# The last mixer's output weights: low halves by a VectorE subtraction instead of an adding transfer, and loads in another order

## The chip, the cores and the metric

The kernel runs on one core of one Trainium2 chip. The metric is the device time of one execution in microseconds (us), as the median of several runs. All five engines of the core have their own queue of instructions and run beside one another: PE (TensorE, the matmuls), DVE (VectorE), ACT (ScalarE), POOL (GpSimd) and SP (SyncE, which here only starts transfers). Each engine takes its queue in order; an instruction that must wait holds up all that stands behind it on that engine.

## The reference

Two blocks over a sequence of 256 rows of width 1024, all in float32: first a block with a pooling and gated-delta mixer and an MLP, then two layers, one with a spatial gating mixer and one with an RWKV-7 mixer, each followed by a squared-relu MLP of hidden width 4096. The change lies in the last steps of the RWKV-7 mixer:

```python
def _rwkv7_mixer(h, mu, w_rkv, ..., ln_g, ln_b, w_o, v_first, v_mix):
    ...                                             # r, k, v, decay, a, g from projections of h
    y = _wkv7_scan(r_h, heads(decay), k_h, v_h, kk, kk * heads(a))   # state recurrence over time
    y = (y - mean(y)) * rsqrt(var(y) + GN_EPS)      # per head of 64
    y = y * ln_g + ln_b
    bonus = sum(r_h * k_h * r_k, axis=-1) * v_h
    y = (y + bonus) * g
    return y @ w_o                                  # [256, 1024] x [1024, 1024]

x = x + y;  x = x + _squared_relu_mlp(_rmsnorm(x, g_ffn), w1, w2);  return _rmsnorm(x, final_g)
```

## The kernel before

A matmul that must be exact in float32 is made of three passes: each operand is split into a high half (a cast to float32r on ACT) and a low half (the rest), and `mm3` (lines 225 to 227) issues high x high, low x high and high x low into the same PSUM bank. So a weight tile of 128x1024 is ready only when its low half is.

There are two ways to make a low half. `split` (line 213 casts, line 217 subtracts) has DVE compute `src - high`. With `lo="x"`, and in `w_out`, `rest` does it instead: ACT writes `-high` into the low tile (line 221), and a transfer that POOL issues adds the raw weights to it (line 222).

`rwkv` holds the mixer. Four windows of 64 time steps (w = 0 to 3) and two halves of the heads (hb = 0, 1) are worked through in five steps: `step(s, fills)` runs `state` (lines 1637 to 1661), `solve` (lines 1669, 1671), `update` (lines 1679 to 1687) and `output` (lines 1693, 1697) of window s for hb = 0 and of window s - 1 for hb = 1, and calls the functions in `fills[0..3]` after state, solve, update and output. These functions are what else there is to do: `fin(d, n)` (the normalisation and gating of row tile d, column half n, lines 1705 to 1718, ended by the four transposes and the split in `half_xt`, lines 246 to 250), `gate_in(n)` (load of the gate weights and of two vectors, lines 1561 to 1564), `gate(n, t)` (their matmuls and products, lines 1575 to 1577), `w_out` (one 128-row tile of the output weights) and `out_mm(t, k, first)` (the output product of row tile t with weight tile k; PSUM tile `ra`).

`w_out` is called eight times, k = 0 to 7. At even k it starts the load of two tiles (`load_as`, line 184, 1 MB) into a raw tile. Raw tiles (`raw`) take turns in two buffers, with those of `gate_in`, so that a load starts when the last reader of the raw tile two before it is done. Each k then has a home for its halves: the pool `wz` for k = 0 and 1 (behind the v weights, whose matmuls are `v`), the tiles `gain` and `sq` for k = 2, the tile `lv` for k = 3 and 4 (it holds the window matrices of w = 0 and 1, last read by `output` of window 1 in step 2), the tile `EL` for k = 5 (last read by `update` of window 1, step 2), `mix` for k = 6 (last read by `update` of window 2, step 3) and `lx` for k = 7 (last read by `output` of window 2, step 3). In the rows all of k = 2, 5 and 6 are called `wo`, k = 0 and 1 `rwoh` and `rwol`, and the raw tiles `rwo`.

The order on each engine is fixed when the program is built: a planner takes the calls in the order of the code as their priority, and pulls a later one forward where it holds that one ready earlier. So the matmuls of `out_mm` and `gate` stand among those of the recurrence on PE, and all casts among the copies of the recurrence on ACT.

After step 4, `early` adds the product to the residual (`add_res`, line 343), the sums are transposed (`m3x`, line 379) and split (lines 382, 385), and the last MLP starts with the matmuls `m3h`; its weights (`m3u`, `m3d`) go through the same raw buffers and through memory that the mixer leaves.

Of the kernel before, what the change touches and what calls it, by code (L numbers as in the profile page):

```python
# [10 lines left out]
F32 = mybir.dt.float32  # L11
# [113 lines left out]
def tile_two_blocks(ctx: ExitStack, tc: tile.TileContext, a: dict):  # L125
    nc = tc.nc
    act, dve, pool, pe, sync = nc.scalar, nc.vector, nc.gpsimd, nc.tensor, nc.sync
# [36 lines left out]
    def acc(i, name):  # L164
        return pa.tile([P, 1024], F32, tag=f"acc{i}", name=name)
# [4 lines left out]
    def raw(name):  # L170
        wpick[1] += 1
        w_ = extra[-1][1] if extra and extra[-1][1] and wpick[1] % 2 and not wpick[2] else wr
        return w_.tile([P, 2048], F32, tag="raw", name=name)
# [22 lines left out]
    def split(src, name, lo=dve, at=None, of=None):  # L196
        shape = list(src.shape)
        n = 1
        for s in shape[1:]:
            n *= s  # L200
        if at is None:
            wpick[0] += 1
            w_ = of or (extra[-1][0] if extra and wpick[0] % 2 and not wpick[2] else wp)
            h = w_.tile([P, 1024], F32R, tag="wh", name=name + "h")
            l = w_.tile([P, 1024], F32R, tag="wl", name=name + "l")
        else:
            x = area(at, [2, D], F32R)
            h, l = x[:, 0], x[:, 1]
        hv, lv = h[:, :n], l[:, :n]
        if len(shape) == 3:  # L210
            hv = hv.rearrange("p (a b) -> p a b", a=shape[1])
            lv = lv.rearrange("p (a b) -> p a b", a=shape[1])
        act.copy(hv, src)  # L213
        if lo == "x":
            rest(lv, hv, src)
        else:
            lo.tensor_tensor(out=lv, in0=src, in1=hv.bitcast(F32), op=ALU.subtract)  # L217
        return hv, lv

    def rest(lv, hv, src):  # L220
        act.activation(out=lv, in_=hv.bitcast(F32), func=AF.Copy, scale=-1.0)
        pool.dma_start(out=lv.bitcast(F32), in_=src, accum_op=ALU.add)

    def mm3(out, lh, ll, rh, rl, first, last):
        pe.matmul(out, lhsT=lh, rhs=rh, start=first, stop=False)  # L225
        pe.matmul(out, lhsT=lh, rhs=rl, start=False, stop=False)  # L226
        pe.matmul(out, lhsT=ll, rhs=rh, start=False, stop=last)  # L227
# [913 lines left out]
    def rwkv(fed, early, cols, mu, hcol, hka, laf):  # L1141
        NP, CH = 8, 64
        half = 0.5 * DECAY
        with tc.tile_pool(name="wz", bufs=2) as wz, tc.tile_pool(name="rw", bufs=1) as bp:
# [75 lines left out]
            with tc.tile_pool(name="rwm2", bufs=2) as m2, tc.tile_pool(name="rwm", bufs=1) as mp:  # L1220
# [288 lines left out]
                def dense():  # L1509
                    for c in (2, 3):  # L1510
                        yield from r_proj(c)
                    q2 = ps("bon")
                    for k in range(NK):
                        for t in range(2):
                            o = t * 16 + k * 2
                            pe.matmul(q2[:, o:o + 2], lhsT=pr[:, k, t * P:(t + 1) * P], rhs=sel[:, k],
                                      start=True, stop=True)
                    dve.tensor_copy(bon.rearrange("p t k -> p (t k)"), q2[:, :32])
                    G1 = xp.tile([P, NK * (T + 1)], F32, tag="xh", name="G1", bufs=2)
                    V1 = xp.tile([P, NK * (T + 1)], F32, tag="xl", name="V1", bufs=2)  # L1520
                    G1, V1 = [x[:, :2 * D].rearrange("p (t m) -> p t m", t=2) for x in (G1, V1)]
                    ac = [acc(t, f"v{t}") for t in range(2)]
                    gv.extend((G1, V1, ac))
                    for k, t in v_proj(0):
                        yield 1
                        if t == 0:
                            gram(k // 2, k % 2)
                            continue
                        if k < 6:
                            turn_bk(k // 2, k % 2)  # L1530
                    v_out(0)
# [13 lines left out]
                def v_out(n):  # L1545
                    G1, V1, ac = gv
                    m = slice(n * 512, n * 512 + 512)
                    for t in range(2):
                        act.copy(DV[0][0:64, t, m], ac[t][0:64, m])
                        act.copy(DV[1][64:128, t, m], ac[t][64:128, m])  # L1550
                        dve.tensor_tensor(out=V1[:, t, m].rearrange("p (h v) -> p h v", v=64),
                                          in0=ac[t][:, m].rearrange("p (h v) -> p h v", v=64),
                                          in1=bon[:, t, 8 * n:8 * n + 8].unsqueeze(2).to_broadcast([P, 8, 64]),
                                          op=ALU.mult)
# [3 lines left out]
                def gate_in(n):  # L1558
                    s = slice(512 * n, 512 * n + 512)
                    w = raw(f"gb{n}")  # L1560
                    sync.dma_start(out=w[:, 0:512], in_=a["rwkv_g_lora_b_2"][0][:, s])
                    lng, lnb = w[:, 512:1024], w[:, 1024:1536]
                    sync.dma_start(out=lng, in_=a["rwkv_ln_g_2"][0][s].partition_broadcast(P))
                    sync.dma_start(out=lnb, in_=a["rwkv_ln_b_2"][0][s].partition_broadcast(P))
                    gates[n] = (lng, lnb) + split(w[:, 0:512], "lgb", of=wp)

                def gate(n, t):
                    G1, V1, _ = gv
                    s = slice(512 * n, 512 * n + 512)
                    lng, lnb, wh, wl = gates[n]  # L1570
                    if not t:
                        gates["q"] = acc(0, "lg")
                    q = gates["q"][:, 512 * t:512 * t + 512]
                    mm3(q, gfh[:, t * P:(t + 1) * P], gfl[:, t * P:(t + 1) * P], wh, wl, True, True)
                    EN[KP["vl"][2 * n + t]].tensor_tensor(out=V1[:, t, s], in0=V1[:, t, s], in1=lnb, op=ALU.add)
                    dve.tensor_mul(V1[:, t, s], V1[:, t, s], q)
                    dve.tensor_mul(G1[:, t, s], lng, q)

                gv = []
                early_fill, late_fill = dense(), v_proj(1)  # L1580
# [141 lines left out]
                wo, wo_raw, lw = [], [], []  # L1722
# [24 lines left out]
                def w_out():  # L1747
                    k = len(wo)
                    if k % 2 == 0:
                        wo_raw.append(load_as(a["rwkv_w_o_2"][0], k * P, f"rwo{k}"))  # L1750
                    w = wo_raw[-1][:, k % 2]
                    if homes[k] is None:
                        wo.append(split(w, "rwo", "x", of=wz))
                    else:
                        h, l = homes[k]()
                        act.copy(h, w)
                        rest(l, h, w)
                        wo.append((h, l))

                def out_mm(t, k, first):  # L1760
# [5 lines left out]
                def step(s, fills):  # L1766
                    todo = [(w, hb) for hb, w in ((0, s), (1, s - 1)) if 0 <= w < 4]
                    for i, stage in enumerate((state, solve, update)):
                        for x in todo:
                            stage(*x)  # L1770
                        for f in fills[i]:
                            f()
                    output(todo)
                    for f in fills[3]:
                        f()
                    todo = [(w + 1, hb) for w, hb in todo if w < 3] + [(0, 1)] * (s == 0)
                    if todo:
                        before(todo)

                c0, c1 = corners(0), corners(1)  # L1780
                some = lambda g, n=1: [lambda: next(g, None)] * n
                rest_of = lambda g: [lambda: [None for _ in g]]
                for _ in c0:
                    next(late_fill, None)
                before([(0, 0)])
                both_fill = [some(c1, 2) + some(late_fill, 2)] * 3
                step(0, both_fill + [rest_of(c1) + rest_of(late_fill) + [lambda: v_out(1), lambda: gate_in(0)]])
                yh, yl = xt_tiles("y")
                f00, f01, f10, f11 = [fin(d, n) for d in both for n in both]
                step(1, [[lambda: gate(0, 0)], [lambda: gate(0, 1), lambda: gate_in(1)], [w_out], [w_out]])  # L1790
                step(2, [some(f00) + [lambda: gate(1, 0)], some(f00) + [lambda: gate(1, 1)],
                         some(f00) + [w_out], some(f00)])
                step(3, [some(f01) + [w_out], some(f01) + [w_out], some(f01) + [w_out], some(f01) + [w_out, w_out]])
                ac = [acc(0, "ra0")]
                outs = lambda t, ks, first: [lambda k=k: out_mm(t, k, first) for k in ks]
                step(4, [some(f10) + outs(0, [0], 0), some(f10) + outs(0, [1], 0), [], some(f10) + outs(0, [2], 0)])
# [21 lines left out]
    with tc.tile_pool(name="lp", bufs=1) as lp:  # L1818

        def area(tag, shape, dt=F32):  # L1820
            return lp.tile([P] + shape, dt, tag=tag, name=tag)
# [83 lines left out]
```

## Time and profile before

| | |
|---|---|
| median of 3 runs | 1082.83 us (1080.8 to 1084.26) |
| profiled execution, its own time | 1082.16 us |
| its span, first to last instruction | 1080.4 us |
| granted TensorE clock, mean | 0.983 |
| busy: PE, DVE, ACT, POOL | 1043.5, 716.3, 567.3, 59.0 us |
| moved by transfers that add (q0) | 8.39 MB in 2304 packets |

Times in the rows are in us from the start of the span unless marked ns. A timeline row gives start, duration, engine, line, operation, what it writes and reads, and in brackets how long the engine had been idle before it and what ended that. In the chain of work each piece is what the next one waited for. A granted clock of 1.00 is TensorE at 2.4 GHz, 0.50 is 1.2 GHz; a value between is a mean over a stretch with both.

### The profile page before, as it was taken

The page shows a single profiled execution, that of the slowest core. Times are in us where ns is not written, and L with a number is a line of the kernel's source. Part 1 is how long each engine was busy: PE and PEld are TensorE (multiplying, and loading weights), DVE is VectorE, ACT ScalarE, POOL GpSimd, SP SyncE. Part 2 cuts the span into 40 slices and gives each one's busy share as a digit, 9 for nine tenths or more (in the row PEclk, how much of TensorE's full clock was granted, in tenths as well). Part 3 has the DMA queues.
Part 4 walks back from the last instruction along what each step waited for, and adds up shares of the span by engine and source line. Part 5 has one row for each costly group of instructions (what it writes and reads, how often), then busy time and mean ns, then how long its engine had stood idle before and what let it go on. Part 6 is the DMA issues. An engine that isn't in the chain of part 4 may idle for free.

```text
span 1080.4 us, 18579 instructions
## 1 busy us (share of the span) xinstructions
PE 1043.5 (97%) x7626; PEld 932.3 (86%) x7626; DVE 716.3 (66%) x1201; ACT 567.3 (53%) x840; POOL 59.0 (5%) x94
## 2 busy tenths in 40 slices
PE   8999999999999999999999999999999789999996
PEld 6899878988899999889989998998777569999985
DVE  5989665555658886666685556998936465555565
ACT  5744464454456554555464546864656445444452
POOL 3100000000002000000000001022001100000000
PEclk9999999999999999999999999999999799999999
DMA  8343186555565645556575561456624874566531
GB/s 247 120 157 118 46 314 214 182 181 177 174 198 153 197 155 174 178 166 190 161 248 188 191 192 36 109 148 142 152 50 118 188 221 159 192 195 187 187 134 39
DMA packets 124465, 177.76 MB, mean 165 GB/s; under 512 B 6766, under 2 KB 100955, under 8 KB 124124
## 3 DMA queue, kind: packets, MB, share of 16 engines
q1 hardware_dynamic: 121930, 168.11, 49.0%
q0 software_dynamic: 2304, 8.39, 4.1%
q8 instruction: 60, 0.98, 0.4%
q14 instruction: 25, 0.20, 0.1%
q10 hardware_dynamic: 146, 0.07, 0.0%
HBM read 167.12 MB, written 1.05 MB: 156 GB/s over the span
## 4 chain that ended last, share of the span: by engine, by line
PE 82%; DVE 9%; DMA 4%; ACT 2%; issue 2%; POOL 1%; SPq 0%; ACTq 0%; POOLq 0%; DVEq 0%
PE m3h L227 3%; PE m3h L226 3%; PE m1a L225 3%; PE m3h L225 3%; PE m1a L227 3%; PE m1a L226 3%; PE m1h L226 3%; PE m2h L226 3%; PE m1h L227 3%; PE m2h L227 3%; PE m1h L225 3%; PE m2h L225 3%; PE m2a L225 3%; PE m2a L226 3%; PE m2a L227 3%; PE m3a L225 3%
## 5 line engine op out<-in xcount | busy, mean ns | idle before, releaser
L225 PE MATMUL m3h<-m3xh,m3uh 128*128 128x256 f32 x256 | 72.6, 284 | 1.9 <-ACT m3xh L382 1.9
L227 PE MATMUL m3h<-m3xh,m3ul 128*128 128x256 f32 x256 | 73.0, 285 | 0.5 <-DVE m3ul L217 0.5
L225 PE MATMUL m1h<-m1xh,m1uh 128*128 128x256 f32 x256 | 73.4, 287 | 0.0
L217 DVE TENSOR_TENSOR m3ul<-m3u,m3uh 128x1024 fp32r<-128x1024 f32 x32 | 39.2, 1226 | 51.1 <-ACT m3uh L213 51.1
L226 PE MATMUL m3h<-m3xl,m3uh 128*128 128x256 f32 x256 | 73.0, 285 | 0.0
L226 PE MATMUL m1h<-m1xl,m1uh 128*128 128x256 f32 x256 | 71.8, 281 | 0.2 <-DVE m1xl L385 0.2
L227 PE MATMUL m2h<-m2xh,m2ul 128*128 128x256 f32 x256 | 71.7, 280 | 0.0
L227 PE MATMUL m1h<-m1xh,m1ul 128*128 128x256 f32 x256 | 71.7, 280 | 0.0
L226 PE MATMUL m2h<-m2xl,m2uh 128*128 128x256 f32 x256 | 71.6, 280 | 0.0
L225 PE MATMUL m2h<-m2xh,m2uh 128*128 128x256 f32 x256 | 71.5, 280 | 0.0
L217 DVE TENSOR_TENSOR m1ul<-m1u,m1uh 128x1024 fp32r<-128x1024 f32 x32 | 39.2, 1225 | 45.1 <-ACT m1uh L213 45.0
L213 ACT CAST m3uh<-m3u 128x1024 fp32r<-128x1024 f32 x32 | 33.4, 1047 | 56.5 <-PE m3h L226 50.7
L217 DVE TENSOR_TENSOR m2ul<-m2u,m2uh 128x1024 fp32r<-128x1024 f32 x32 | 39.1, 1225 | 35.8 <-ACT m2uh L213 35.8
L213 ACT CAST m1uh<-m1u 128x1024 fp32r<-128x1024 f32 x32 | 33.7, 1053 | 52.3 <-PE m1h L226 50.5
L213 ACT CAST m2uh<-m2u 128x1024 fp32r<-128x1024 f32 x32 | 33.5, 1050 | 47.9 <-PE m2h L226 45.8
L217 DVE TENSOR_TENSOR m2dl<-m2d,m2dh 128x1024 fp32r<-128x1024 f32 x32 | 39.2, 1225 | 26.1 <-ACT m2dh L213 26.1
L217 DVE TENSOR_TENSOR m3dl<-m3d,m3dh 128x1024 fp32r<-128x1024 f32 x31 | 38.0, 1225 | 24.9 <-ACT m3dh L213 24.9
L217 DVE TENSOR_TENSOR m1dl<-m1d,m1dh 128x1024 fp32r<-128x1024 f32 x31 | 37.9, 1224 | 22.0 <-ACT m1dh L213 22.0
L225 PEld LDWEIGHTS m3h<-m3xh,m3uh 128*128 128x128 f32 x256 | 49.0, 192 | 2.8 <-ACT m3xh L382 2.2
L213 ACT CAST m2dh<-m2d 128x1024 fp32r<-128x1024 f32 x32 | 33.6, 1050 | 33.4 <-PE m2a L227 29.9
L213 ACT CAST m1dh<-m1d 128x1024 fp32r<-128x1024 f32 x31 | 32.5, 1047 | 35.3 <-PE m1a L227 24.4
L213 ACT CAST m3dh<-m3d 128x1024 fp32r<-128x1024 f32 x31 | 32.6, 1052 | 33.4 <-PE m3a L227 31.6
(691 smaller groups left out, 3513.4 us busy)
## 6 DMA issues: line engine op xcount, KB each, us to landing
m1u<-in_w_up_dram SPq DMA_DIRECT2D x16, 1024.0 KB, 5.5
m1d<-in_w_down_dram SPq DMA_DIRECT2D x16, 1024.0 KB, 5.0
m2u<-in_ffn_w_dram SPq DMA_DIRECT2D x16, 1024.0 KB, 6.4
m2d<-in_ffn_w_dram SPq DMA_DIRECT2D x16, 1024.0 KB, 5.2
m3u<-in_ffn_w_dram SPq DMA_DIRECT2D x16, 1024.0 KB, 5.5
m3d<-in_ffn_w_dram SPq DMA_DIRECT2D x16, 1024.0 KB, 5.1
win<-in_w_in_dram SPq DMA_DIRECT2D x10, 1024.0 KB, 5.3
sv<-in_sgu_w_in_dram SPq DMA_DIRECT2D x8, 1024.0 KB, 5.8
```

Of the source, the lines that this page charges most:

```text
L213: act.copy(hv, src)
L217: lo.tensor_tensor(out=lv, in0=src, in1=hv.bitcast(F32), op=ALU.subtract)
L225: pe.matmul(out, lhsT=lh, rhs=rh, start=first, stop=False)
L226: pe.matmul(out, lhsT=lh, rhs=rl, start=False, stop=False)
L227: pe.matmul(out, lhsT=ll, rhs=rh, start=False, stop=last)
```

## The change

Two lines change how the eight low halves are made, and the lists of fills change when `w_out` is called:

```diff
-                        wo.append(split(w, "rwo", "x", of=wz))
+                        wo.append(split(w, "rwo", of=wz))
                     else:
                         h, l = homes[k]()
                         act.copy(h, w)
-                        rest(l, h, w)
+                        dve.tensor_sub(l, w, h.bitcast(F32))
                         wo.append((h, l))
...
-                step(0, both_fill + [rest_of(c1) + rest_of(late_fill) + [lambda: v_out(1), lambda: gate_in(0)]])
+                step(0, both_fill + [rest_of(c1) + rest_of(late_fill) + [lambda: v_out(1), lambda: gate_in(0), w_out, w_out]])
...
-                step(1, [[lambda: gate(0, 0)], [lambda: gate(0, 1), lambda: gate_in(1)], [w_out], [w_out]])
-                step(2, [some(f00) + [lambda: gate(1, 0)], some(f00) + [lambda: gate(1, 1)],
-                         some(f00) + [w_out], some(f00)])
-                step(3, [some(f01) + [w_out], some(f01) + [w_out], some(f01) + [w_out], some(f01) + [w_out, w_out]])
+                step(1, [[lambda: gate(0, 0)], [lambda: gate(0, 1), lambda: gate_in(1)], [w_out], []])
+                step(2, [some(f00) + [lambda: gate(1, 0)], some(f00) + [lambda: gate(1, 1)], some(f00), some(f00) + [w_out]])
+                step(3, [some(f01) + [w_out], some(f01) + [w_out], some(f01), some(f01) + [w_out, w_out]])
```

By k: before, k = 0 and 1 come after update and output of step 1, k = 2 after update of step 2, and k = 3 to 7 in step 3 (one each after state, solve and update, two after output). After the change k = 0 and 1 come after output of step 0, k = 2 after update of step 1, k = 3 after output of step 2, k = 4 and 5 after state and solve of step 3, k = 6 and 7 after its output. With that the raw tiles follow one another as gate 0, weights 0 and 1, gate 1, weights 2 and 3, 4 and 5, 6 and 7; before, both gates came first.

## Rows read from the trace of the kernel before

**Rows 1.** Page, part 4: shares of the chain of work, by engine

```profile
PE 82%; DVE 9%; DMA 4%; ACT 2%; issue 2%; POOL 1%; SPq 0%; ACTq 0%; POOLq 0%; DVEq 0%
```

**Rows 2.** Windows: length; busy PE, PEld, DVE, ACT, POOL; clock; DMA share; GB/s

```profile
805.00:840.00 35.00, 33.39 (x413) 27.12 (x414) 21.94 (x52) 21.90 (x35) 4.53 (x5) 1.00 0.44 102
840.00:848.60 8.60, 3.64 (x37) 2.82 (x32) 2.23 (x4) 3.37 (x4) 0.02 (x1) 1.00 0.81 201
848.60:867.10 18.50, 16.81 (x79) 12.21 (x77) 7.21 (x18) 8.85 (x13) 3.44 (x4) 0.54 0.84 199
867.10:889.50 22.40, 17.90 (x82) 13.16 (x82) 16.18 (x36) 9.57 (x21) 0.00 (x0) 1.00 0.74 236
889.50:893.10 3.60, 3.60 (x20) 3.60 (x18) 2.13 (x10) 2.18 (x6) 0.00 (x0) 0.53 0.00 0
```

**Rows 3.** Chain of work from 838 to 885: start, us, what

```profile
838.10 9.53 DMA lv<-rwo
...
859.87 10.59 DMA lx<-rwo
...
877.87 7.01 DMA m3u<-in_ffn_w_dram
```

**Rows 4.** Timeline of PE: waits for low halves, recurrence groups, a gate matmul

```profile
815.02 0.50 PE L225 MATMUL lg<-lgbh,gfh 128*128 128x512 f32 x1
...
826.99 1.10 PE L1693 MATMUL PD<-tBK,lv 128*64 128x64 f32 x16
...
840.13 0.92 PE L1693 MATMUL PD<-tBK,lx 128*64 128x64 f32 x13
842.58 0.50 PE L226 MATMUL ra<-wo,yh 128*128 128x512 f32 x1 [1.52 <-DMA wo<-rwo]
...
847.67 0.50 PE L226 MATMUL ra<-lv,yh 128*128 128x512 f32 x1 [3.44 <-DMA lv<-rwo]
```

**Rows 5.** Timeline of ACT: casts and negations among the recurrence's copies

```profile
807.07 0.58 ACT L1661 COPY xx<-PD 64x512 f32<-64x512 f32 x1
...
821.46 1.99 ACT L213 CAST rwoh<-rwo 128x1024 fp32r<-128x1024 f32 x2
823.36 2.00 ACT L221 ACTIVATE rwol<-rwoh 128x1024 fp32r<-128x1024 f32 x2
...
845.23 1.04 ACT L1756 CAST lv<-rwo 128x1024 fp32r<-128x1024 f32 x1 [6.56 <-DMA rwo<-in_rwkv_w_o_dram]
...
849.15 1.19 ACT L1697 COPY tBK<-PD 64x512 f32<-64x512 f32 x2
```

**Rows 6.** Groups by line, 800 to 890: count, busy us, mean ns, idle before

```profile
L221 ACT ACTIVATE wo<-wo 128x1024 fp32r<-128x1024 f32 x3 | 3.1, 1049 | 0.0
...
L217 DVE TENSOR_TENSOR m3ul<-m3u,m3uh 128x1024 fp32r<-128x1024 f32 x3 | 3.7, 1224 | 3.4 <-ACT m3uh L213 3.4
```

**Rows 7.** Transfers by issue, 725 to 900: count, KB each, median us to landing

```profile
wo<-rwo POOLq DMA_DIRECT2D x3, 512.0 KB, 9.1
...
rwo<-in_rwkv_w_o_dram SPq DMA_DIRECT2D x4, 1024.0 KB, 6.7
...
gb<-in_rwkv_g_lora_b_dram SPq DMA_DIRECT2D x2, 256.0 KB, 2.6
```

**Rows 8.** Timeline of SP's queue: a gate load, the first two weight loads

```profile
793.46 0.33 SPq L1561 DMA_DIRECT2D gb<-in_rwkv_g_lora_b_dram  x1
...
814.46 0.38 SPq L184 DMA_DIRECT2D rwo<-in_rwkv_w_o_dram  x1
...
825.07 0.38 SPq L184 DMA_DIRECT2D rwo<-in_rwkv_w_o_dram  x1
```

**Rows 9.** Timeline of DVE: the second gate weights' low half; the last fin

```profile
800.45 0.69 DVE L217 TENSOR_TENSOR lgbl<-gb,lgbh 128x512 fp32r<-128x512 f32 x1
...
867.22 0.69 DVE L1705 TENSOR_REDUCE gm<-tBK 128x8 f32<-128x512 f32 x1 [0.56 <-ACT tBK L1697]
...
878.37 0.69 DVE L250 TENSOR_TENSOR yl<-yt,yh 128x512 fp32r<-128x512 f32 x1 [1.37 <-ACT yh L249]
```

## Prediction, written before the changed kernel was timed

> **What bounds the kernel now.** I read the shares of the chain of work first: PE holds 82% of it [rows 1], so time is won where PE waits or runs slowly, and nowhere else. Then the windows around the last mixer's end [rows 2], cut where the clock changes. From 805 to 840 us PE is busy 33.39 of 35.00 us: nothing to win there but 1.61. From 840.0 to 848.6 it is busy 3.64 of 8.60, and from 848.6 to 867.1 it is busy 16.81 of 18.50 but at a granted clock of 0.54, mostly 1.2 GHz. From 867.1 to 889.5 it is busy 17.90 of 22.40 at full clock, and from 889.5 to 893.1 the clock is at 0.53 again [rows 2]. So two kinds of loss stand side by side:
> - waits from 840.0 to 867.1: 8.60 - 3.64 + 18.50 - 16.81 = 6.65 us;
> - the low clock: 16.81 us of work that at full clock would be 16.81 x 0.54 = 9.1, so 7.7 us; and 3.60 x 0.47 = 1.7 in the short stretch at 889.5.
>
> Third, the chain and the timelines say what ended the waits. The chain runs through two adding transfers, 9.53 and 10.59 us from POOL's issue to landing [rows 3]. PE stood 1.52 and 3.44 us before the first matmul that reads a low half [rows 4]. ACT stood 6.56 us before the cast of k = 4, for a load whose raw buffer was still being read by the adding transfers of k = 0 and 1; behind that cast stood the copies of step 3's output, which ran at 849.15 although their matmuls were done by 841.05 (840.13 + 0.92) [rows 4, 5]. So step 4 of the recurrence began 8 us late on account of the weights. After 867.22 the last `fin` takes to 879.06 (878.37 + 0.69) [rows 9], with PE short of work at its end; this is a chain of small steps that the change leaves.
>
> **The change part by part.** *Removed:* eight ACT negations, 8 x 1.049 = 8.4 us [rows 6]; eight adding transfers, each about 9.1 us from issue to landing [rows 7]. *Added:* eight DVE subtractions of the same shape as those of the MLP's weights, 8 x 1.224 = 9.8 us [rows 6]. A low half now follows its cast by 1.2 us, instead of a negation, an issue and a transfer, 1.05 + 9.1 us and more. Also the raw buffer is free after the subtraction, so the next load no longer waits for the adding transfer.
>
> *Moved, by k.* The load of k = 0 and 1 takes the place that the second gate load had in the buffers, so it starts at about 793.46 [rows 8] and is there by 800.2 (6.7 us to landing [rows 7]). Its halves must wait for the v matmuls, to about 805, and are done near 809. The load of k = 2 and 3 can start when these are done or behind the gate load on SP's queue, near 815 instead of 825.07 [rows 8]; k = 2 is ready near 825. k = 3 must wait for its home until 826.99 + 1.10 = 828.1 [rows 4]. The load of k = 4 and 5 waits for the gates' last product, about where the load at 825.07 started [rows 8], or a few us later; it lands near 835. That of k = 6 and 7 follows the subtraction of k = 3, near 831, and lands near 839; their homes come free at 840 to 841 [rows 4]. So all eight low halves are there by about 846, where the last one before landed at 859.87 + 10.59 = 870.46 [rows 3]. Then neither PE's waits for low halves nor ACT's wait of 6.56 has a cause left.
>
> *What is late next.* From 841 on there are two limits. One is PE's own work: 3.64 + 9.1 + 17.90 = 30.6 us at full clock for what lay between 840.0 and 889.5 [rows 2], which would end at 870.6. The other is the chain: from 841.05 the two copies of output, 1.19; state's matmuls, about 2.7 (an estimate from 1.10 for a group of 16 [rows 4], for 16 such and 8 wider ones); then copy, solve, copy, output, copy, 3 x 0.58 + 2 x 1.1 [rows 4, 5], with hand-overs of 0.1: about 849.4; the last `fin`, 11.84 us from its start to its end before [rows 9], at 861; the last product, then the sums, transposes and splits. This too comes to about 871. Two limits that close together don't hide each other fully: of the 6.65 + (22.40 - 17.90) = 11.15 us of waits I leave 4.2, most of it in the tail.
>
> *What is added to the path.* Four terms that the trace of before doesn't show:
> - The casts of k = 0 and 1 now stand at about 805, ahead of the copy that ACT began at 807.07 [rows 5] and that the recurrence waits for. Cost 0 to 2.0 us (two casts, the 1.99 of [rows 5]); I take 1.0, since PE had other matmuls to run. The place they leave, 821.46 to 825.36 [rows 5], gives ACT 4 us, which PE, full there, can hardly use: 0 to -1.6, taken as 0.
> - The second gate load now waits for the first gate's buffer, to 814.46, where before it was issued at 793.46 [rows 8]. Landing 2.6 [rows 7], a cast and a subtraction of 0.69 [rows 9] bring its low half near 818.5 to 819.5, where PE reached its first gate matmul at 815.02 [rows 4]. Behind that matmul the recurrence of step 2 is queued on PE, and behind the product on DVE the state's additions. Cost 0 to 4.5; I take 0.5, because these matmuls can stand later in PE's order at no loss.
> - The subtractions of the last three k fall among the small DVE steps of the last two `fin`: 0 to 3 x 1.224 = 3.7; I take 0.5, since DVE was busy only 9.44 of the 27.10 us from 840.0 to 867.1 [rows 2].
> - The loads start earlier and meet less other traffic: 0.
>
> *Sum.* Waits 11.15 - 4.2 = 6.95; low clock 7.7; half of the 1.7 at 889.5, as that stretch follows a wait of PE that I only shorten: 0.85; less 2.0 for the added terms: 13.5 us. The profiled execution took 1082.16, which is 0.67 under the median of the runs; the sum is made against the former: 1082.2 - 13.5 = 1068.7.
>
> On the clock there is a rule to weigh. The 7.7 us rest on a low clock through 848.6 to 867.1, though PE was busy 16.81 of 18.50 us there [rows 2]. The Trainium skill, "TensorE: Matmul & The Clock Gate", section "What's actually happening", says that the engine is throttled by default and activity releases it; by that the clock should have come back early in this stretch, and the term would be near 0 and the sum 5.8. The trace shows the low clock lasting, so the measured term stands.
>
> **The rivals.**
> 1. *The clock falls all the same.* Short waits of PE remain between 840 and 870 (the chain's four stations, the `fin`), and the trace shows that a busy engine can be held at 1.2 GHz. Then the 7.7 stay lost: gain 5.8, 1076.4. For it: the second fall at 889.5 came after a stretch with only 4.5 us of waits in 22.4 [rows 2]. Against it: the long one followed 4.96 us of waits in 8.60.
> 2. *The wait moves to the loads.* If the load of k = 4 and 5 lands late again and ACT's order keeps the cast ahead of the copies, the 6.56 us [rows 5] come back, and with them the low clock: 13.5 - 6.56 - 7.7 = -0.8, no change, 1083. For it: each raw buffer still waits for a reader, and SP takes its queue in order. Against it: the readers are now 1.2 us subtractions, and the load has some 10 us more.
> 3. *Slower: the gate's wait brings the clock down early.* If PE keeps its gate matmul at 815 and stands 4.5 us for the gate weights, with the recurrence behind it, the clock may fall there, in a stretch where PE has no slack (33.39 of 35.00 busy [rows 2]). Each us at 0.54 costs 0.46. With 4.5 for the wait it takes back the 13.5 when the low clock lasts (13.5 - 4.5) / 0.46 = 20 us; the one seen lasted 18.5. From 818 to 848 it would cost 4.5 + 13.8 = 18.3, so 4.8 slower, 1087. Against it: it needs a longer fall than any seen here, from a shorter wait.
> 4. *DVE becomes the limit.* All eight subtractions on the path cost 9.8 instead of 0.5: gain 4.2, 1078. DVE's 21.94 of 35.00 busy before 840 [rows 2] leaves room; only runs of small steps with a copy waiting behind them would show it.
>
> **How the numbers follow.** The forecast's own range: at best only 2 us of waits stay and the added terms cost nothing, 11.15 - 2 + 7.7 + 1.7 = 18.5, 1063.7; at worst the added terms cost their upper ends, 2.0 + 4.5 + 3.7 = 10.2 in place of 2.0, gain 5.3, 1077. Chances: forecast 0.64, rival 1 0.12, rival 2 0.06, rival 3 0.05, rival 4 0.06, a gain over 18.5 us 0.07. The range from 1063 to 1077.5 holds the forecast and rival 1 and leaves out the others. Some 0.3%, 3.2 us, is what a measurement of this kernel can tell from no change: all cases but rivals 2 and 3 lie beyond it with a little to spare, so faster 0.88, the same 0.06, slower 0.06.
>
> **What would show it.** In the changed kernel's profile: no adding transfers of `rwo`, POOL idle there; PE's waits before `ra` matmuls named by DVE or ACT, not by a DMA, and each under 1 us; the output copies of step 3 on ACT within 2 us of their matmuls; a granted clock of 1.00 from 840 on; `m3h` beginning 13 to 17 us earlier, with the whole of the MLP behind it as long as before. Wrong would be: a wait of ACT or DVE for `rwo` or `gb` of several us, PE standing before `lg`, a clock near 0.5 anywhere from 815 to 870, or a last `fin` that takes much longer than 11.84 us with subtractions inside.

## The result, and the profile after

The changed kernel takes 1070.1 us (median of 4 runs, 1068.24 to 1071.05) beside 1082.17 of the kernel before in the same rounds: a ratio of 0.9881, 95% interval 0.9865 to 0.9898, so 12.1 us faster. In a second round of runs the same kernel gave 1070.52 (ratio 0.9871, 0.9833 to 0.9909). The profiled execution took 1070.76 us with a span of 1069.0, 11.4 less than the span of before. The forecast was 1068.7.

The page of the changed kernel, DMA queues (q0 is the queue of the transfers that add) and shares of the chain of work:

```profile
q0 software_dynamic: 1152, 4.19, 2.1%
...
PE 84%; DVE 10%; ACT 2%; issue 1%; DMA 1%; POOL 0%; SPq 0%; ACTq 0%; DVEq 0%; POOLq 0%
```

Half of the bytes that adding transfers moved are gone, and DMA's share of the chain fell from 4% to 1% [rows 1]. That is the wait which the change was to remove, and it is removed. The windows of the changed kernel, cut where waits and clock change (length; busy PE; clock; DMA share; GB/s):

```profile
805.00:831.35 26.35, 25.76 (x335) 1.00 0.33 112
831.35:835.04 3.69, 0.00 (x0) 0.87 0.77 275
835.04:844.45 9.41, 9.41 (x73) 0.51 0.38 113
844.45:869.80 25.35, 24.44 (x159) 1.00 0.29 95
869.80:880.00 10.20, 8.68 (x47) 1.00 0.67 232
880.00:890.00 10.00, 9.53 (x79) 1.00 0.26 71
```

Beside [rows 2]: the waits with their 8.60 us stretch and the 18.50 us at 0.54 have become one standstill of 3.69 us, in which PE does nothing at all, and 9.41 us at 0.51, in which it is never idle. The second fall of the clock, at 889.5 us before, has gone. What PE waited for from 805 to 895 us (in total, how often, longest):

```profile
PE yt L246 <- DVE tBK L1718: 3.7, 1, 3.7
PE ra L225 <- DVE res L343: 0.8, 1, 0.8
...
PE ra L227 <- DVE yl L250: 0.5, 1, 0.5
PE ra L225 <- ACT yh L249: 0.4, 1, 0.4
```

No DMA is among them; before, PE stood 1.52 and 3.44 us for adding transfers [rows 4]. The one large wait is new: the transposes of the first `fin` (row tile 0, first half) wait for its last step (L1718, an addition). PE's timeline at that place:

```profile
835.04 1.09 PE L246 MATMUL yt<-ident,tBK 128*128 128x128 f32 x4 [3.69 <-DVE tBK L1718]
836.06 3.44 PE L1669 MATMUL Ud<-xx,TT 64*64 64x64 f32 x32
```

The matmuls of step 3's solve stand behind the four transposes on PE, so the recurrence waits too, and then runs at half speed: 32 matmuls take 3.44 us.

**Where the 11.4 us of the span came from.** The first `m3h` is the same point in both kernels. From 805 us up to it, first the kernel before, then the changed one:

```profile
805.00:888.33 83.33, 70.81 (x594) 0.90 0.65 171
805.00:878.68 73.68, 67.34 (x600) 0.93 0.40 133
```

PE waited 12.5 us before and 6.3 after; that is 6.2. Low clock: before 7.7 + 1.7 = 9.4 (the 1.7 lie behind the first `m3h`), after 9.41 x 0.49 = 4.6; that is 4.8. Together 11.0; the other 0.4 these windows don't assign.

### The profile page after: what moved, and what is told of

Same layout as the page of the kernel before. It is cut to its first block, busy times and chain, and to the rows that moved or that the text cites. A ratio compares the mean times of both kernels' runs of the same rounds, so it can differ in the third digit from the quotient of the medians.

```text
span 1069.0 us, 18564 instructions
## 1 busy us (share of the span) xinstructions
PE 1038.1 (97%) x7626; PEld 930.1 (87%) x7626; DVE 722.8 (68%) x1209; ACT 559.5 (52%) x832; POOL 51.8 (5%) x86
## 3 DMA queue, kind: packets, MB, share of 16 engines
HBM read 167.12 MB, written 1.05 MB: 157 GB/s over the span
## 4 chain that ended last, share of the span: by engine, by line
PE 84%; DVE 10%; ACT 2%; issue 1%; DMA 1%; POOL 0%; SPq 0%; ACTq 0%; DVEq 0%; POOLq 0%
PE m1a L225 3%; PE m3h L226 3%; PE m3h L227 3%; PE m1a L227 3%; PE m1a L226 3%; PE m3h L225 3%; PE m1h L226 3%; PE m2h L226 3%; PE m2h L227 3%; PE m1h L227 3%; PE m1h L225 3%; PE m2h L225 3%; PE m2a L225 3%; PE m2a L226 3%; PE m2a L227 3%; PE m3a L225 3%
## 5 line engine op out<-in xcount | busy, mean ns | idle before, releaser
L225 PE MATMUL m2a<-m2dh,m2fh 128*128 128x512 f32 x128 | 50.1, 391 | 0.0
```

## The experiments

Each ratio is to the kernel before, run on the same chip in the same rounds. Timeline rows below have the columns of the rows ahead of the prediction.

### Each half of the change alone

`e1_sub_only` keeps the lists of before and takes only the subtractions; `e2_order_only` takes only the new lists and keeps negation and adding transfer.

```diff
# e1_sub_only, against before
-                        wo.append(split(w, "rwo", "x", of=wz))
+                        wo.append(split(w, "rwo", of=wz))
...
-                        rest(l, h, w)
+                        dve.tensor_sub(l, w, h.bitcast(F32))
# e2_order_only, against after
-                        wo.append(split(w, "rwo", of=wz))
+                        wo.append(split(w, "rwo", "x", of=wz))
...
-                        dve.tensor_sub(l, w, h.bitcast(F32))
+                        rest(l, h, w)
```

Expected of the subtractions alone:

> The subtraction alone: low halves on VectorE, the calls of w_out in the old order. Theory A (the cost was the time from a cast to its low half, and the raw buffers that the adding transfers held): the load of k = 4 and 5 starts near 825 instead of 837, no engine waits over 2 us for a load of rwo, PE's waits before ra go from DMA to DVE, and most of the gain is there: 7 to 12 us under the kernel before. Theory B (the loads came too late, whatever makes the low half; the order carries the gain): under 4 us gained, with ACT still standing 4 us or more for rwo.

Expected of the order alone:

> The order alone: the calls of w_out moved as in the change, low halves still by adding transfers. Theory A: the raw buffers are still held for about 9 us by the transfers, so the load of k = 6 and 7 starts near 840 and the last low half lands near 858 instead of 870; 3 to 7 us gained, the clock still low for 10 us or more after 840. Theory B: 8 to 12 us gained, since the loads start 15 to 20 us earlier.

Measured: subtractions alone 1073.12 us (0.9926, 0.9900 to 0.9952), order alone 1073.24 (0.9916, 0.9883 to 0.9948). By these ratios each alone brings 8 or 9 us; both together bring 13 or 14 by theirs (0.9881 and 0.9871). Of the subtractions theory A held (7 to 12 us expected), of the order theory B (8 to 12), so neither theory alone is the account. The two gains don't add up: either half takes the weights off the critical path nearly whole, and what is left then is much the same for both, a `fin` that PE waits for and a low clock after it. In the profile of either half the clock is near 0.5 twice: from about 836 to 843 us in both, and again from 856 to 860 (subtractions alone) or from 863 to 870 (order alone). PE's longest waits, first of the subtractions alone, from 805 to 895 us:

```profile
PE yt L246 <- DVE gt L273: 3.0, 1, 3.0
```

and of the order alone, where one adding transfer still shows:

```profile
PE yt L246 <- DVE tBK L1718: 2.3, 1, 2.3
...
PE ra L226 <- DMA lx<-rwo: 1.2, 1, 1.2
```

### Is it the subtractions on DVE? Three ways to move them

In the changed kernel the subtraction of k = 4 stands between the first `fin`'s second product (L1717) and its last step (L1718), and that of k = 3 among its small steps. DVE's timeline of the changed kernel:

```profile
828.84 1.22 DVE L1757 TENSOR_TENSOR lv<-rwo,lv 128x1024 fp32r<-128x1024 f32 x1 [0.31 <-ACT lv L1756]
...
830.85 0.69 DVE L1716 TENSOR_TENSOR tBK<-tBK,gr 128x512 f32<-128x512 f32 x1
...
832.06 0.68 DVE L1717 TENSOR_TENSOR tBK<-tBK,G 128x512 f32<-128x512 f32 x1
833.07 1.23 DVE L1757 TENSOR_TENSOR lv<-rwo,lv 128x1024 fp32r<-128x1024 f32 x1 [0.32 <-ACT lv L1756]
834.21 0.69 DVE L1718 TENSOR_TENSOR tBK<-tBK,V 128x512 f32<-128x512 f32 x1
```

Theory A took these two for the cause. `e4_pool` puts the subtractions of k = 2 to 7 on GpSimd:

```diff
-                        dve.tensor_sub(l, w, h.bitcast(F32))
+                        pool.tensor_sub(l, w, h.bitcast(F32))
```

> The changed kernel with the subtractions of k = 2 to 7 on GpSimd instead of VectorE. In the changed kernel PE stands 3.69 us before the first yt transposes, with the recurrence's solve behind them, and its clock is low for the next 9.4 us. Theory A (the subtractions of k = 2 to 4 stand among the steps of the first fin on VectorE and delay them): the wait falls under 1.5 us, the clock stays at full, and the time is 4 to 8 us under the changed kernel, near 1062 to 1066, if a GpSimd subtraction takes no more than 3 us. Theory C (that fin is late for its own chain and the gate products, not for the subtractions): the wait stays over 2.5 us and the time within 2 us of the changed kernel.

Measured: 1077.64 us (0.9953, 0.9929 to 0.9977), 7 us more than the changed kernel. GpSimd takes 2.34 to 2.80 us for one, and the two DVE steps below that begin right behind its start end 0.03 and 0.55 us after it does. GpSimd's timeline, then DVE's:

```profile
829.25 2.34 POOL L1757 TENSOR_TENSOR lv<-rwo,lv 128x1024 fp32r<-128x1024 f32 x1 [4.19 <-ACT lv L1756]
834.08 2.35 POOL L1757 TENSOR_TENSOR lv<-rwo,lv 128x1024 fp32r<-128x1024 f32 x1 [2.49 <-ACT lv L1756]
```

```profile
829.34 2.28 DVE L1706 TENSOR_SCALAR gm<-gm 128x8 f32<-128x8 f32 x1
...
834.19 2.79 DVE L1718 TENSOR_TENSOR tBK<-tBK,V 128x512 f32<-128x512 f32 x1
```

A step of 8 columns that takes 0.17 us elsewhere took 2.28 here, and L1718 2.79 in place of 0.69; PE's wait before `yt` grew to 6.1 us. So this run says nothing for or against theory A: it took the subtractions away and put a longer hold in their place. The Trainium skill, "SBUF — State Buffer", section "SBUF: two separate sides", says that VectorE and GpSimd share a pair of memory ports: of a GpSimd instruction and a VectorE instruction that needs the pair (one with two SBUF inputs, or in a two-port mode), whichever starts first holds it for its whole length, and the other is blocked. The times of the two pairs of rows agree.

`e6_hold` and `e7_hold_yl` leave them on DVE and set those of k = 3, 4 and 5 behind the first `fin`, behind its last step or behind its `yl`:

```diff
# e6_hold; e7_hold_yl takes the instruction of L250 in place of that of L1718
-                    dve.tensor_add(Y, Y, V1[:, d, hs])
+                    lastfin[d, n] = dve.tensor_add(Y, Y, V1[:, d, hs])
...
-                        dve.tensor_sub(l, w, h.bitcast(F32))
+                        with tc.issue_after(lastfin[0, 0].ins) if k in (3, 4, 5) else ExitStack(): dve.tensor_sub(l, w, h.bitcast(F32))
```

> The changed kernel with one constraint more: the three subtractions of weights 3, 4 and 5 stand on VectorE behind the last small product (L1718) of the first fin; buffers, loads and everything on TensorE are as in the changed kernel. Theory A (the two subtractions that ran among the small steps of the first fin, 2 x 1.22 us, made its tBK late; TensorE's queue holds the solve behind that transpose, and the low clock follows from the standstill): the wait of TensorE ahead of yt falls from 3.7 us to under 1.5, no clock near 0.5 between 831 and 845 us, and the time is 4 to 8 us under that of the changed kernel (1062 to 1066). Theory C (the fin is late by its own chain and the gate's products, whatever stands among them): the wait stays above 2.5 us, the low clock stays, and the time is within 2 us of the changed kernel. Rival to both: the weights' low halves come late, and TensorE waits ahead of ra on VectorE for over 2 us: as slow as the changed kernel, by another wait.

> As the run before, but the three subtractions stand behind the first fin's yl (L250), one 0.69 us step and what it waits for further on. Theory A: the same gain, 4 to 8 us under the changed kernel; the wait of TensorE ahead of yt under 1.5 us; the weights' low halves some 2 us later than in the run before, which the products ra pay for with at most 1 us of waiting. Theory C: within 2 us of the changed kernel, the wait ahead of yt above 2.5 us.

`e3_no_low` drops the six subtractions:

```diff
-                        dve.tensor_sub(l, w, h.bitcast(F32))
-                        wo.append((h, l))
+                        wo.append((h, h))
```

> Left out: the low halves of weights 2 to 7; the products take the high half in both places, so TensorE has the same work and VectorE six subtractions (6 x 1.22 = 7.3 us) less. It measures what the six subtractions cost in all. Theory A: 5 to 9 us under the changed kernel (1061 to 1065), no wait over 1.5 us ahead of yt, clock 1.00 from 831 to 870 us. Theory C: within 2 us of the changed kernel.

The control in the same rounds:

> The changed kernel once more, on the same chip and in the same rounds as the three others: 1068 to 1072 us, a wait of TensorE ahead of yt of about 3.7 us, and the clock near 0.5 behind it.

Measured, in the order of the expectations: 1075.12 (0.9906, 0.9873 to 0.9940), 1074.84 (0.9902, 0.9869 to 0.9935) and 1069.96 us (0.9861, 0.9823 to 0.9898), beside 1070.52 for the changed kernel again. Theory A fell. The two holds were even some 4 us slower than the control, in times that overlap with its (1071.63 to 1078.60 beside 1068.32 to 1076.07): in their profiles PE stands a second time, 1.47 and 2.75 us before the second `fin`'s transposes, and the clock falls a second time, near 866 and 864 us. Even with 7.3 us of subtractions taken out of DVE the time hardly moves, and the standstill stays, as the windows of `e3_no_low` show:

```profile
832.70:835.50 2.80, 0.07 (x2) 1.00 0.88 344
835.50:843.80 8.30, 8.30 (x57) 0.59 0.43 128
```

What takes the place of the subtraction is seen in DVE's timeline of `e6_hold`:

```profile
831.72 0.69 DVE L1717 TENSOR_TENSOR tBK<-tBK,G 128x512 f32<-128x512 f32 x1
833.73 0.69 DVE L1712 TENSOR_REDUCE gv<-hT 128x8 f32<-128x512 f32 x1 [1.31 <-ACT hT L1710]
834.33 0.68 DVE L1718 TENSOR_TENSOR tBK<-tBK,V 128x512 f32<-128x512 f32 x1
```

Ahead of the first `fin`'s last step stands a reduction of the second `fin`, which waits for ScalarE; and ScalarE does that step only after the recurrence's copy at L1661. Of the 3.69 us the subtraction of k = 4 was worth one: 2.73 remained.

### Does a shorter first wait help? It comes back at the second fin

`e5_yt_late` calls the four transposes only after the solve of step 3; `e8_hold_fin` is `e6_hold` and also sets the second `fin`'s reduction behind the first `fin`'s last step; `e9_hold_k2` moves cast and subtraction of k = 2 behind it as well:

```diff
# e5_yt_late, against after (step 2 without its last some(f00))
-                step(3, [some(f01) + [w_out], some(f01) + [w_out], some(f01), some(f01) + [w_out, w_out]])
+                step(3, [some(f01) + [w_out], some(f00) + some(f01) + [w_out], some(f01), some(f01) + [w_out, w_out]])
# e8_hold_fin, against e6_hold
-                    dve.tensor_reduce(var, ysq, AX.X, ALU.add)
+                    with tc.issue_after(lastfin[0, 0].ins) if (d, n) == (0, 1) else ExitStack(): dve.tensor_reduce(var, ysq, AX.X, ALU.add)
# e9_hold_k2, against e8_hold_fin: step 1 only starts the load of k = 2 and 3; w_out for k = 2 after update of step 2
-                        with tc.issue_after(lastfin[0, 0].ins) if k in (3, 4, 5) else ExitStack(): dve.tensor_sub(l, w, h.bitcast(F32))
+                        with tc.issue_after(lastfin[0, 0].ins) if k in (2, 3, 4, 5) else ExitStack(): dve.tensor_sub(l, w, h.bitcast(F32))
```

> The changed kernel with only the last part of the first fin (its transposes and split) called after solve of step 3 instead of after output of step 2, so that on PE the transposes no longer stand ahead of the solve. Theory A (the wait of 3.69 us and the low clock behind it are lost because PE takes its queue in order): neither is there any more, and the time is 3 to 8 us under the changed kernel. Theory D (PE has no other work ready at that point, so the idle time only moves): as much idle time and a low clock between 828 and 850, and the time within 2 us of the changed kernel or above it.

> The changed kernel, with the subtractions of weights 3, 4 and 5 and also the reduction of the second fin (L1712, which waits for ScalarE) put behind the first fin's last product (L1718) on VectorE. Theory F (VectorE works in order, and the first fin's last step stands behind steps that are not its own: a subtraction, 1.0 us, and, once that is gone, the second fin's reduction, whose operand comes late from ScalarE, 1.9 us): the wait of TensorE ahead of yt falls from 3.7 us to under 1.2. Theory H (the low clock is what follows a standstill): with that short a wait no stretch near 0.5 between 831 and 845 us, and the time 4 to 6 us under that of the changed kernel (1064 to 1067 us). Rival J (the low clock has another cause than the standstill): the clock is near 0.5 behind yt all the same, and the time is within 2 us of the changed kernel.

> As the run before, and the cast and the subtraction of weight 2 (1.04 us on ScalarE, 1.22 us on VectorE) also come behind the first fin's products; the load of weights 2 and 3 stays where it was. Theory F: the first fin's chain is some 2 us shorter, and TensorE doesn't wait ahead of yt at all (under 0.4 us). Theory H: clock 1.00 from 831 to 845 us, 1062 to 1066 us. Rival J: low clock all the same, within 2 us of the changed kernel. A rival of its own: the halves of weights 2 to 5 now come in one row behind the first fin, 4 x 1.2 us, and TensorE waits over 2 us ahead of ra for them; then as slow as the changed kernel.

Measured: `e5_yt_late` 1071.08 us (0.9899, 0.9863 to 0.9935), `e8_hold_fin` 1072.99 (0.9918, 0.9890 to 0.9946), `e9_hold_k2` 1072.86 (0.9922, 0.9899 to 0.9945). On the wait theory F held: 3.69, then 2.73 without the subtraction, 0.86 without the reduction too, and none in `e9_hold_k2`. The time fell in none of them. Nor did theory H's sign come in `e8_hold_fin`, where the clock was to stay up behind so short a wait. It fell twice all the same, after waits of 0.45 and 0.22 us for the gate weights at 814 us, and after 0.86 and 1.26 us at 832 to 836:

```profile
817.00:819.00 2.00, 2.00 (x14) 0.57 0.38 154
819.00:821.00 2.00, 2.00 (x12) 0.58 0.00 0
...
837.40:841.20 3.80, 3.80 (x40) 0.55 0.61 185
```

So that run speaks for rival J, a low clock of another cause, as much as for theory H. The waits of `e9_hold_k2`, 805 to 905 us, and its windows:

```profile
PE yt L246 <- DVE gt L274: 2.8, 1, 2.8
PE m3x L379 <- DVE m3im L302: 2.4, 1, 2.4
```

```profile
831.00:847.60 16.60, 15.26 (x141) 1.00 0.47 148
847.60:850.40 2.80, 0.06 (x1) 1.00 0.63 257
850.40:858.00 7.60, 7.00 (x46) 0.63 0.42 138
```

Here the clock stays up where it fell before; the standstill has moved by 15 us, from the transposes of the first `fin` to those of the second, and the low clock with it. On DVE the second `fin` now meets what was moved out of the first one's way, and splits of the MLP's weights as well:

```profile
846.66 1.22 DVE L217 TENSOR_TENSOR m3ul<-m3u,m3uh 128x1024 fp32r<-128x1024 f32 x1
847.79 0.68 DVE L1717 TENSOR_TENSOR tBK<-tBK,G 128x512 f32<-128x512 f32 x1
...
848.47 1.22 DVE L217 TENSOR_TENSOR m3ul<-m3u,m3uh 128x1024 fp32r<-128x1024 f32 x1
849.61 0.68 DVE L1718 TENSOR_TENSOR tBK<-tBK,V 128x512 f32<-128x512 f32 x1
```

The waits as a whole didn't shrink with the first one. From 805 us up to the first `m3h`, `e8_hold_fin` and then `e9_hold_k2`:

```profile
805.00:877.86 72.86, 64.63 (x592) 0.95 0.41 134
805.00:880.19 75.19, 66.60 (x601) 0.95 0.40 130
```

PE waited 8.2 and 8.6 us, and in `e6_hold` and `e7_hold_yl` 7.8 and 8.4, where the changed kernel waited 6.3. In `e5_yt_late` the wait before `yt` was 1.86 us, with 0.56 more behind it, and the clock was low behind it for 10 us; PE stood 2.35 us more before `m3h`, for ScalarE (6.1 us of waits in all):

```profile
835.94 0.63 PE L246 MATMUL yt<-ident,tBK 128*128 128x128 f32 x4 [1.86 <-DVE tBK L1718]
```

```profile
837.00:847.30 10.30, 9.74 (x44) 0.50 0.64 204
```

That is its theory D: idle time and low clock only moved. In seven profiles in which the weights are no longer late (the changed kernel, `e3_no_low` and `e5_yt_late` to `e9_hold_k2`) `m3h` began between 876.4 and 882.8 us, whichever wait was the long one.

### Does the low clock come from the standstill? Work for nobody in its place

`e12_fill` fills the standstill with 22 transposes of the identity that nothing reads. `e14_fill_gate` has 28 of them, and also holds the second gate's first products behind step 2's state:

```diff
# e12_fill, against after; the four transposes are called after step 3's state, and its solve is held behind them
-        q = bank(name)
+        q = [bank(name)]; fill(q[1:] or q); q = q[0]
...
-                gv = []
+                gv, busy = [], lambda q: [after_own(lambda: pe.transpose(q[0][:, :P], ident, ident)) for _ in range(22)]
# e14_fill_gate, against e12_fill, with range(28)
-                    mm3(q, gfh[:, t * P:(t + 1) * P], gfl[:, t * P:(t + 1) * P], wh, wl, True, True)
+                    with tc.issue_after(pd["o"].ins) if n and not t else ExitStack(): mm3(q, gfh[:, t * P:(t + 1) * P], gfl[:, t * P:(t + 1) * P], wh, wl, True, True)
```

> The changed kernel with work that nothing uses: 22 transposes of the identity (128x128), some 3.1 to 3.5 us by the 0.14 to 0.16 us that such a transpose takes at full clock, stand on TensorE between the state of step 3 and the first fin's four transposes, in the place of the standstill; the solve of step 3 is kept behind those four, as in the changed kernel; nothing else that comes before them moves. The wait itself can't get shorter by it. Theory H: the rest of the wait is under 0.7 us, the clock stays at 1.00 from 831 to 845 us, and the time falls by 3 to 5 us (1065 to 1067.5). Rival J: the clock falls near 0.5 behind yt all the same, and the time is within 1.5 us of the changed kernel.

> The run with 22 transposes of nothing's use, with 28 of them (some 3.3 us by the 0.12 us each that the 22 took) and one more edit: the second gate's first products come behind step 2's state on TensorE (some 3 us of work), so that its weights, loaded late, have landed by then. Theory H with rival 3 of the prediction (a wait at that gate of 0.7 to 1.1 us puts the clock down in some executions, and that makes the spread of 1067 to 1078 us in the run before; the wait of the first fin does it in all of them): no wait over 0.3 us ahead of lg, clock 1.00 from 805 to 845 us, and the times lie close together at 1064 to 1068 us. Rival J (the clock falls by itself, whatever TensorE waited for): times in two groups again, some of them at 1073 to 1078 us. Rival K (the gate's products, 3 us later, make the first fin later in turn): the wait ahead of yt is over 1.5 us, and the time 1069 us or more.

Measured: `e12_fill` 1071.00 us (0.9899, 0.9861 to 0.9936), `e14_fill_gate` 1071.08 (0.9886, 0.9859 to 0.9913). The medians hide two groups. `e12_fill` gave 1067.02, 1067.20 and 1067.79 at mean granted clocks of 0.990 to 0.992, and 1074.21, 1074.64 and 1078.25 at 0.979 to 0.986; `e14_fill_gate` ran from 1066.51 (0.992) to 1076.55 (0.982). The profiled execution of `e12_fill` is one of the longer ones (1074.64), and its windows show why:

```profile
816.90:818.90 2.00, 1.26 (x5) 1.00 0.93 185
818.90:832.50 13.60, 13.60 (x93) 0.52 0.16 63
832.50:880.00 47.50, 44.39 (x371) 0.99 0.48 156
```

Where the changed kernel has its low clock, this one is at 0.99, with 2.62 us of filling and 1.05 us of waiting before `yt`: at this place theory H's sign came, in one profile. But now the clock is low earlier, for 13.6 us after PE had stood 0.91 and 0.23 us for the second gate weights. The profile of `e14_fill_gate` has no wait for the gate, one of 0.94 us for a copy of ScalarE, and the same again:

```profile
818.40:820.80 2.40, 1.46 (x10) 1.00 0.85 226
820.80:834.50 13.70, 13.70 (x105) 0.53 0.11 46
```

So what `e14_fill_gate` was to show, times close together at 1064 to 1068 us, did not come, and rival K's wait didn't either (0.40 us before `yt`). Times on both sides, 1066.51 to 1069.02 and 1073.14 to 1076.55, are what rival J had expected. In the windows shown here every fall of over 9 us follows a standstill, the shortest of about 1 us; the reverse doesn't hold: `e8_hold_fin` stood 2.28 us before its second `yt` at 852 us and stayed at 1.00. And the 0.45 and 0.22 us for gate weights, after which its clock fell, were 0.46 and 0.22 in `e9_hold_k2`, where it did not. What decides it is open, and theory H is not shown. That the executions at 1067 us had no early fall is read from their mean clocks; none of them was profiled. No kernel that computes the whole had a lower median than the changed kernel; `e5_yt_late`, `e12_fill` and `e14_fill_gate` can't be told apart from it.

## Why the prediction was right

Time, sign and main mechanism came out as forecast: 1070.1 against 1068.7. That the number is so close is partly luck: the low clock gave 3.75 us less than its term, and costs of 2.0 us didn't show. One of the prediction's own signs of being wrong came, a clock near 0.5 between 815 and 870 us, and `m3h` stayed short of its 13 to 17 us.

- **Waits for the weights gone: right.** No PE wait is for a DMA; the last low half was ready at 848.5 us instead of 870.46, where 846 was forecast; the output copies of step 3 ran at 843.01 and 845.73, each straight after its matmuls, and the 6.56 us of ACT [rows 5] are gone. Rival 2 did not come.
- **Waits that stay: 4.2 forecast, too few.** I put them into the tail. In the tail 1.52 us were left, but 3.69 stood at 831 us, where I had looked for nothing.
- **Low clock: 7.7 + 0.85 gained by forecast, 4.8 measured.** This is the term that was mis-sized most. I let it go whole because its wait went; behind a new wait of 3.69 us came 9.41 us at 0.51, and rival 1 came in half. In that stretch PE was never idle. That the wait is its cause is not shown. The rule of the Trainium skill that I weighed ("TensorE: Matmul & The Clock Gate", "What's actually happening": activity releases the throttle) gives a shorter one; here too the measurement decides.
- **Subtractions among the small steps: 0 to 3.7, took 0.5.** I looked at DVE's busy share of the 27 us behind 840, and for the last two `fin`. It was the first one, where DVE holds far more. The one of k = 4 cost 0.96 us of the standstill (3.69 less the 2.73 of `e6_hold`), so the size was near the forecast and the place was not; the subtractions are only one of the late things there. The first `fin` came to its last step at 834.21 us, where before it was there at 828.30, in DVE's timeline of the kernel before:

```profile
819.07 0.69 DVE L1712 TENSOR_REDUCE gv<-hT 128x8 f32<-128x512 f32 x1 [1.36 <-ACT hT L1710]
...
828.30 0.69 DVE L1718 TENSOR_TENSOR tBK<-tBK,V 128x512 f32<-128x512 f32 x1
```

  After the change its square on ACT (L1710, 822.20 against 818.40) stands behind the cast of k = 2, and its reduction (L1712, 823.48 against 819.07) behind the subtraction of k = 2. That is rival 4's mechanism at another place, at the price of a wait.
- **Casts of k = 0 and 1 ahead of a copy: 1.0 taken, and seen for one of the two.** The cast of k = 0 was done at 801; the cast of k = 1 ran at 807.57 us and the copy behind it at 808.64, where it ran at 807.07 before [rows 5]. It cost the sum nothing: PE's waits from 805 to 831 us fell from 0.96 to 0.59 us (before it was busy 25.39 of the same 26.35).
- **Second gate load: 0.5 taken, 0.22 us on PE.** The step that failed here is where its buffer came from. I took that of the first gate, free at 814.46; it took that of weights 0 and 1, free when their second subtraction ended at 811.15. So by these times the raw tiles don't strictly take turns, as the section on the kernel before has it. PE filled most of that time with other work; the chain of work that ended last does run through this load, 3.46 us from 811.17. SP's queue after the change:

```profile
811.17 0.33 SPq L1561 DMA_DIRECT2D gb<-in_rwkv_g_lora_b_dram  x1
...
814.79 15.66 SPq L184 DMA_DIRECT2D rwo<-in_rwkv_w_o_dram  x3
```

  Rival 3, the gate's wait bringing the clock down early, didn't happen in the changed kernel's profile. The profile of `e12_fill` has what it describes: 13.6 us at 0.52 after 1.1 us of waiting for the gate, at 0.48 a us lost that is 6.5, and the two groups of its times lie 7 apart. But `e14_fill_gate`, where PE doesn't wait for the gate, shows the same fall, so the gate is not shown to be the cause.
- **`m3h` 13 to 17 us earlier: 9.7** (878.68 against 888.33); the low clock behind it, 1.7 us, went as well.

Added up: waits 6.2 in place of 6.95 (12.5 less 6.3, from 805 us to the first `m3h`), the low clock 4.8 in place of 8.55, and what the terms for 2.0 cost lies within these waits: 11.0 of the span's 11.4, in place of 13.5.

## What to carry to other kernels

Cut the trace into windows and count waits and low clock apart, and when a wait goes, look for the next one ahead of the old place as well as behind it: here it came 10 us earlier. On an engine that works in order, cost a moved step by who stands behind it there, not by the engine's busy share: of the 3.69 us one was the moved subtraction and nearly two another step's operand from a third engine. If several edits each shorten the standing wait and the time hardly moves, add up all waits of the stretch: here they grew from 6.3 to between 7.8 and 8.6 us in the four runs that held steps back on DVE, while the first one shrank. That a chain of small dependent steps holds the stretch and passes the wait on is my reading of these sums; no run here shortens the whole chain to test it.

## What the runs showed of the hardware

- The low clock lasted 9.41 to 13.7 us with PE busy all the time, after standstills of 3.69 us (changed kernel), 0.91 and 0.23 us (`e12_fill`) and 0.94 us (`e14_fill_gate`). A standstill of 2.28 us passed without it (`e8_hold_fin`), and waits of 0.46 and 0.22 us passed without it in one kernel where 0.45 and 0.22 us in another did not.
- While GpSimd does a 128x1024 subtraction (2.34 us where DVE takes 1.22), a DVE step of 8 columns can take 2.28 us in place of 0.17: moving work from DVE to GpSimd cost 7 us here.
- Transposes of 128x128 that nothing uses took 0.12 us each at full clock (2.62 us for 22), and the clock was at 0.99 over the place where it fell without them, in one profile whose clock had been low until just before; the median time was no lower.
